# Loading the raw A tiles of a Strassen stage 6.5 products ahead instead of 9, in a one-core Mamba-2/GLA layer

## The chip, the cores and the metric

One core of a Trainium2 chip. The metric is the device time of one execution in microseconds, as the median of several runs. The change is judged by whether that time goes down, stays or goes up.

## The reference, cut to what matters

The kernel computes one layer of a hybrid decoder: 2048 tokens and 16 meta tokens in front of them, of width 1024, float32. A root-mean-square norm feeds one wide input projection; from it come a Mamba-2 (SSD) branch with a causal convolution and a chunked scan, a gated linear attention (GLA) branch, and two merge gates. Each branch output goes through a 1024 by 1024 projection, is multiplied by the sigmoid of its gate, and the sum goes through an output projection onto the residual, with a last norm:

```
u = rmsnorm(h, norm_w)
z, xbc, dt, q, k, v, g, a_lr, merge_g = split(u @ w_in)
y_ssd = norm(ssd(conv(xbc), dt) * silu(z))
y_gla = norm(gla(q, k, v, log_sigmoid(a_lr @ w2 + b))) * silu(g)
gates = sigmoid(merge_g)                    # two of them
merged = gates0 * (y_ssd @ w_br0) + gates1 * (y_gla @ w_br1)
out = rmsnorm(h + merged @ w_out, final_norm_w)
```

The last four lines' products, from `merge_g` on, are what the second half of the kernel computes, and where most of the change lies.

## The kernel before, in words

**Number format.** Every float32 operand is split into a high and a low part of the faster type fp32r: ACT copies the raw tile into the high part, and DVE or POOL subtracts it from the raw tile for the low part. A product is then three matmuls, L190 (high by high), L191 and L192 (the cross terms). A tile is not ready for TensorE (PE) until it is loaded (SP issues the DMA), copied (ACT) and subtracted.

**Phase 1 (0 to about 1500 us).** Four blocks of 512 tokens; in each, eight units of input projections (four SSD, four GLA) on PE, with the scans of earlier units run beside them. Weights come through `load_w`: a raw tile `wr` by DMA, ACT L170 for the high part, POOL L171 for the low part, both into `whl`; the first time, the split weight is also stored to DRAM (`k_...`, by `save`), and from then on it is loaded split. In block 0 every weight is split this way. Besides its own weights, block 0 also prepares the six weights of the first gate products (`EARLY`, products 1 and 2 of three column groups), one behind each of the units 0 to 5; they are needed only at the end of phase 1. The order of the instructions of PE and SP is the order of the program here; the other engines' order is set by a planner.

**Phase 2 (about 1525 us to the end).** Seven stages: two of gates (gate1, gate0), four of branches (br00, br10, br01, br11) and the output stage. Each multiplies 2 by 2 blocks with the Winograd form of Strassen's algorithm: seven products P1 to P7, in the order 1, 2, 6, 7, 5, 3, 4, the weights as A and the tokens as B (in the output stage the tokens as A and the weights as B). A stage has four or eight column groups n, taken in pairs: P1 of the even n, P1 of the odd n, P2 of both, and so on, 14 products to a pair. A product is 12 matmuls.

- A: `load_a` (L948) loads four raw tiles `ar` of a group (a11, a21, a22, a12, 256 KB each; eight buffers, so two groups). `sum_a` (L957 to L960) makes the sums on POOL, three into tiles `as` and one over a21. `prep_a` splits what a product needs into `a` (ACT L968, DVE L969). P1, P2 and P4 use raw tiles a11, a12, a22, so a buffer of `ar` is free once the last of its splits is done; a22 is split last, for P4.
- B: `load_b` (L936) loads a raw tile `br` (five buffers), `prep_b` splits it into `b1` to `b7` (ACT L941, DVE L942), 28 tiles per stage.
- Products accumulate in banks: P1, P6, P5, P3 in a bank `pj`, with P1, P6 and P5 each copied out by ACT (`sn`, L989) before the next product enters the same bank. P7 and P4 use `pt`, P2 uses `pc`.
- `fetch` loads gates or partial sums into `io` (L1034, L1038; L1062 in the output stage, where the buffers are first stored as the result), and ACT's queue stores finished tiles (L1158). `make_sums` prepares sums of B for later stages.

SP's order is by hand in phase 2 as well, the order of the other engines is the planner's. The place of a load in SP's order is set by a position counted in products: `at(pos, fn)` puts it down, and after product i the entries of positions i to i+1 are run in order of position. A load stands at `i - LOAD` for the first product i of a group (one product later for odd n). Since the odd group's own first product is one later too, that is 9 products ahead for the even group and 7 behind that pair's start for the odd. The split `prep_a` stands `AHEAD` products in front of its product; the loads of a stage's 28 B tiles begin 16 positions ahead of their stage (12 and 4 more), 0.8 of a position apart.

SP issues loads one after the other, and each waits for its own buffer to be free, so a load that waits holds all loads behind it.

**The passage.** The last phase-1 steps run early products of the first gate stage: P1 and P2 of n = 0, 1, 2 and P6 of n = 0 and 1, from weights and sums kept in SBUF. Then the pools of phase 1 on the right side of SBUF are released, and pools of phase 2 are opened in their place (`bops7`, `bops5`, `raws`, `aops`, `outs`, `small`), so that the first tiles of phase 2 wait for the last uses of phase-1 tiles at the same addresses (among them `acc`, `act`, `cin`, `tok` and `g`). The first entries run at position -1: A of n = 0 and 1, then B of P7 and P5.

```
at(first_at.get(n, i - LOAD + (n % 2)), lambda st=st, n=n: load_sum_a(st, n))
...
def load_sum_a(st, n):
    st.load_a(n)
    st.sum_a(n)
```

## Time and profile before

| | |
|---|---|
| runs | 2344.55, 2331.62, 2341.62 us, median 2341.62 |
| profiled execution | 2336.1 us, span 2334.3 us, mean granted TensorE clock 0.990 |
| PE busy | 2251.8 us, 96% of the span |
| PE weight loads | 1949.7 us, 84% |
| DVE busy | 1556.3 us, 67% |
| ACT busy | 1184.6 us, 51% |
| POOL busy | 696.6 us, 30% |
| DMA moved | 528.56 MB, mean 226 GB/s |

PE matmul and PEld (the weight loads of the array) overlap. A line names an instruction's place in the code, its engine, its output and inputs, how many there were, their busy time and mean duration in ns, and after the bar the idle time of the engine in front of them with what ended most of it. `SPq` rows are the sequencer that issues DMAs, with the time that it waited. In a timeline a row is start, duration, instruction, and in square brackets the idle time before it and what released it. The granted clock is 1.00 at full speed and 0.50 at half.

### The profile page before, as it was taken

The page shows a single profiled execution, that of the slowest core. Times are in us where ns is not written, and L with a number is a line of the kernel's source. Part 1 is how long each engine was busy: PE and PEld are TensorE (multiplying, and loading weights), DVE is VectorE, ACT ScalarE, POOL GpSimd, SP SyncE. Part 2 cuts the span into 40 slices and gives each one's busy share as a digit, 9 for nine tenths or more (in the row PEclk, how much of TensorE's full clock was granted, in tenths as well). Part 3 has the DMA queues.
Part 4 walks back from the last instruction along what each step waited for, and adds up shares of the span by engine and source line. Part 5 has one row for each costly group of instructions (what it writes and reads, how often), then busy time and mean ns, then how long its engine had stood idle before and what let it go on. Part 6 is the DMA issues. An engine that isn't in the chain of part 4 may idle for free.

```text
span 2334.3 us, 36553 instructions
## 1 busy us (share of the span) xinstructions
PE 2251.8 (96%) x12641; PEld 1949.7 (84%) x12641; DVE 1556.3 (67%) x2893; ACT 1184.6 (51%) x2762; POOL 696.6 (30%) x691
## 2 busy tenths in 40 slices
PE   7899999999999999999999999979999999999998
PEld 6899988888889989888988898858788778777786
DVE  5677766676675676576667556655644778887875
ACT  4666655465544455544455534444644644453543
POOL 3444533122222122211212101046354333423241
PEclk9999999999999999999999999989999999999999
DMA  8766966667785676786666656468765778877753
GB/s 297 246 214 227 323 234 206 224 195 240 239 283 186 213 222 213 265 275 201 206 222 217 204 170 200 131 212 257 245 208 183 237 250 285 285 277 246 245 166 110
DMA packets 305579, 528.56 MB, mean 226 GB/s; under 512 B 28144, under 2 KB 144112, under 8 KB 305392
## 3 DMA queue, kind: packets, MB, share of 16 engines
q1 hardware_dynamic: 204432, 413.33, 54.0%
q10 hardware_dynamic: 100960, 112.88, 13.9%
q8 instruction: 99, 1.62, 0.3%
q14 instruction: 88, 0.72, 0.1%
HBM read 375.76 MB, written 150.34 MB: 225 GB/s over the span
## 4 chain that ended last, share of the span: by engine, by line
PE 42%; DMA 12%; DVE 7%; issue 4%; ACT 4%; POOL 2%; SPq 2%; ACTq 0%; POOLq 0%; DVEq 0%
PE pj L190 9%; PE pj L192 9%; PE pj L191 9%; DMA br<-br_t 2%; DVE b L942 2%; PE pt L191 1%; PE pt L192 1%; DVE a L969 1%; PE pt L190 1%; DMA acc<-in_xmt 1%; PE pc L190 1%; PE pc L192 1%; PE pc L191 1%; PE pc L708 1%; DMA io<-g 1%
## 5 line engine op out<-in xcount | busy, mean ns | idle before, releaser
L190 PE MATMUL pj<-u,whl 128*128 128x512 f32 (+1 forms) x1196 | 453.6, 379 | 15.3 <-ACT g_all L442 6.2
L192 PE MATMUL pj<-u,whl 128*128 128x512 f32 (+1 forms) x1196 | 437.4, 366 | 1.1 <-POOL whl L171 0.6
L191 PE MATMUL pj<-u,whl 128*128 128x512 f32 (+1 forms) x1196 | 436.2, 365 | 0.0
L190 PE MATMUL pj<-whl,u 128*128 128x256 f32 (+1 forms) x992 | 289.3, 292 | 2.0 <-ACT u L303 2.0
L192 PE MATMUL pj<-whl,u 128*128 128x256 f32 (+1 forms) x992 | 282.7, 285 | 1.4 <-DVE u L305 1.4
L191 PE MATMUL pj<-whl,u 128*128 128x256 f32 (+1 forms) x992 | 282.5, 285 | 0.2 <-POOL whl L171 0.2
L190 PEld LDWEIGHTS pj<-u,whl 128*128 128x128 f32 x1196 | 228.9, 191 | 54.1 <-ACT acc L480 7.1
L192 PEld LDWEIGHTS pj<-u,whl 128*128 128x128 f32 x1196 | 228.4, 191 | 37.8 <-POOL whl L171 1.6
L191 PEld LDWEIGHTS pj<-u,whl 128*128 128x128 f32 x1196 | 229.2, 192 | 33.7
L190 PE MATMUL pj<-b,a 128*128 128x512 f32 x620 | 242.9, 396 | 10.5 <-ACT sn L989 9.1
L192 PE MATMUL pj<-b,a 128*128 128x512 f32 x620 | 243.9, 394 | 3.0 <-DVE a L969 3.0
L191 PE MATMUL pj<-b,a 128*128 128x512 f32 x620 | 244.1, 394 | 1.0 <-DVE b L942 1.0
L171 POOL TENSOR_TENSOR whl<-wr,whl 128x512 fp32r<-128x512 f32 (+1 forms) x106 | 142.9, 1356 | 184.3 <-ACT whl L170 146.0
L942 DVE TENSOR_TENSOR b<-br,b 128x512 fp32r<-128x512 f32 x196 | 157.7, 828 | 59.2 <-ACT b L941 56.0
L190 PEld LDWEIGHTS pj<-whl,u 128*128 128x128 f32 x992 | 190.1, 192 | 3.4 <-ACT u L303 2.6
L80 POOL TENSOR_TENSOR wr<-wr 128x256 f32<-128x256 f32 x80 | 65.8, 822 | 425.9 <-DMA wr<-u 172.8
L192 PEld LDWEIGHTS pj<-whl,u 128*128 128x128 f32 x992 | 190.0, 192 | 1.9 <-DVE u L305 1.9
L191 PEld LDWEIGHTS pj<-whl,u 128*128 128x128 f32 x992 | 190.3, 192 | 0.9 <-POOL whl L171 0.4
L957 POOL TENSOR_TENSOR as<-ar,ar 128x512 f32<-128x512 f32 x40 | 63.2, 1580 | 405.0 <-DMA ar<-in_w_br 192.7
L969 DVE TENSOR_TENSOR a<-ar,a 128x512 fp32r<-128x512 f32 x154 | 133.0, 878 | 75.6 <-ACT a L968 74.9
L941 ACT ACTIVATE b<-br 128x512 fp32r<-128x512 f32 x196 | 119.9, 627 | 119.1 <-DMA br<-br_t 46.0
L484 DVE SCALAR_TENSOR_TENSOR acc<-cin,hcw,acc 128x512 f32<-128x512 f32 (+1 forms) x192 | 153.8, 801 | 30.0 <-ACT acc L480 29.1
(290 smaller groups left out, 5061.2 us busy)
## 6 DMA issues: line engine op xcount, KB each, us to landing
whl<-k_s SPq DMA_DIRECT2D x96, 512.0 KB, 4.3
whl<-k_g SPq DMA_DIRECT2D x96, 512.0 KB, 4.1
whl<-k_v SPq DMA_DIRECT2D x48, 512.0 KB, 3.8
wr<-in_w_feat SPq DMA_DIRECT2D x72, 256.0 KB, 4.3
whl<-k_z SPq DMA_DIRECT2D x36, 512.0 KB, 3.7
k_s<-whl SPq DMA_DIRECT2D x32, 512.0 KB, 3.7
cb<-cumd ACTq DMA_DIRECT2D x64, 256.0 KB, 5.5
y<-gg ACTq DMA_DIRECT2D x64, 256.0 KB, 4.4
```

The lines of the kernel that those rows point to most:

```text
L80: nc.gpsimd.tensor_tensor(o, x, y, op=ALU.subtract)
L171: nc.gpsimd.tensor_tensor(hl[:, 1], raw, hl[:, 0].bitcast(F32), op=ALU.subtract)
L190: nc.tensor.matmul(ps, sh, mh, start=first, stop=False, **kw)
L191: nc.tensor.matmul(ps, sh, ml, start=False, stop=False, **kw)
L192: nc.tensor.matmul(ps, sl, mh, start=False, stop=last, **kw)
L484: nc.vector.scalar_tensor_tensor(acc, cin[:, k:k + tt], hcw[:, ti, k:k + 1], acc, op0=ALU.mult, op1=ALU.add)
L708: nc.tensor.matmul(ps[:, r * P:(r + 1) * P], kq[:, 2 * r * P:(2 * r + 1) * P], kq[:, (2 * r + 1) * P:(2 * r + 2) * P], start=True, stop=True)
L941: nc.scalar.activation(t[:, 0], raw, AF.Copy)
L942: nc.vector.tensor_tensor(t[:, 1], raw, t[:, 0].bitcast(F32), op=ALU.subtract)
L957: nc.gpsimd.tensor_tensor(s1, a21, a22, op=ALU.add)
L969: nc.vector.tensor_tensor(t[:, 1], src, t[:, 0].bitcast(F32), op=ALU.subtract)
```

## The change

Four edits. First, in block 0 the six early gate weights come behind units 2 to 7 instead of units 0 to 5. Second, tiles `as` move from the pool `raws` to a pool of their own (`sums`), and tiles `io` from the pool `outs` to a pool of their own (`ios`), both opened ahead of `raws`; the same numbers of buffers. By that the tiles lie at other addresses: `io` over phase 1's `acc`, `cb`, `c1` and `cin`, `ar` over `act` and `cin` (before, over `acc` and `cb`), and the first five `a` where `io` and a part of `a` lay; `as` stay. Third, LOAD becomes 6.5, so that a group's raw tiles of A are placed 6.5 products (even n) ahead of the pair's first product or 4.5 (odd n) instead of 9 and 7. Since `prep_a` of P4, in front by AHEAD = 5, is placed at 7 and 6 products ahead of the pair's first product, the load of A now stands behind the split of a22, in the order of the program, and not in front of it. Fourth, in the first gate stage the four B tiles of P7 are placed ahead of A of n = 0 and 1.

The number of instructions on every engine stays the same, and so does PE's order in phase 1. In phase 2 the groups of four loads of A move on SP: at a stage's start three loads of B (the tenth to twelfth) come in front of the even group and three more in front of the odd group, and in places two fetches of `io` or four loads of `make_sums` too.

```diff
@@ phase 1, block 0
-            if b == 0 and i < len(EARLY):
-                load_w(*gate_w(*EARLY[i]))
+            if b == 0 and i >= 2:
+                load_w(*gate_w(*EARLY[i - 2]))
@@ sum_a
-            s1, s2, s4 = [mk(rpl, [P, 4, P], F32, "as", bufs=6) for _ in range(3)]
+            s1, s2, s4 = [mk(asl, [P, 4, P], F32, "as", bufs=6) for _ in range(3)]
@@ io
-        return mk(opl, [P, BLK], F32, "io", bufs=8)
+        return mk(iol, [P, BLK], F32, "io", bufs=8)
@@ the order of phase 2
-    AHEAD, LOAD = 5, 9
+    AHEAD, LOAD = 5, 6.5
...
-            first_at = {0: -1, 1: -0.99, 3: 2, 2: 3} if st is stages[0] else {}
+            first_at = {0: -0.99, 1: -0.985, 3: 2, 2: 3} if st is stages[0] else {}
...
-    begins_b = {7: -0.98, 5: -0.9, 3: 0.5, 4: 1.8, 1: 3.2, 2: 4.4, 6: 5.6}
+    begins_b = {7: -1, 5: -0.9, 3: 0.5, 4: 1.8, 1: 3.2, 2: 4.4, 6: 5.6}
@@ make_sums of later stages
-                        yield from make_sums(opl, "io", 8, *sums[key], j, c, nc.scalar)
+                        yield from make_sums(iol, "io", 8, *sums[key], j, c, nc.scalar)
@@ the pools of phase 2
+    asl, iol = pool2("sums", 1, side="right"), pool2("ios", 1, side="right")
     rpl = pool2("raws", 1, side="right")
```

Lines behind 1182 of the changed kernel are one further down.

## The prediction

> **What bounds the kernel now.** I read the engines' busy times first, then the stretches, then the waits, and only then the instructions around the waits that cost something.

> The page, its span, its engine table and two groups of matmuls:

> ```profile
> span 2334.3 us, 36553 instructions
> PE 2251.8 (96%) x12641; PEld 1949.7 (84%) x12641; DVE 1556.3 (67%) x2893; ACT 1184.6 (51%) x2762; POOL 696.6 (30%) x691
> L190 PE MATMUL pj<-u,whl 128*128 128x512 f32 (+1 forms) x1196 | 453.6, 379 | 15.3 <-ACT g_all L442 6.2
> L190 PE MATMUL pj<-b,a 128*128 128x512 f32 x620 | 242.9, 396 | 10.5 <-ACT sn L989 9.1
> ```

> TensorE is the bound: 2334.3 - 2251.8 = 82.5 us are idle. The change removes no matmul, so it can win back only idle time and time at the halved clock. The stretches where it acts (columns: length, busy time of each engine, granted clock, DMA share, GB/s):

> ```profile
> 103.00:116.30 13.30, 10.40 (x78) 9.66 (x79) 12.48 (x26) 7.74 (x21) 7.14 (x8) 1.00 0.69 226
> 116.30:119.70 3.40, 3.40 (x17) 3.40 (x17) 0.97 (x3) 1.98 (x4) 0.13 (x1) 0.50 0.82 275
> 1536.20:1546.40 10.20, 4.49 (x8) 2.35 (x9) 6.58 (x5) 4.41 (x7) 10.04 (x8) 0.50 0.70 248
> 1550.00:1578.00 28.00, 24.87 (x96) 18.54 (x97) 22.68 (x30) 17.80 (x34) 12.34 (x8) 0.94 0.75 253
> 1600.00:2200.00 600.00, 588.13 (x2528) 473.49 (x2527) 424.27 (x571) 295.14 (x531) 234.79 (x180) 1.00 0.74 248
> ```

> Three places: block 0 (an idle of some 3 us and 3.4 us at half clock behind it), the passage from phase 1 to phase 2 at 1525 to 1578, and the 600 us of stages with 11.9 us idle. What TensorE waits for between 1600 and 2200 is nearly all of that 11.9:

> ```profile
> PE pj L190 <- ACT sn L989: 8.7, 10, 2.2
> PE pj L192 <- DVE a L969: 3.0, 3, 1.4
> ```

> A product may not enter the pj bank until ACT has copied the one before out of it (the snapshot, L989). So I asked what ACT waits for from 1600 on, and what SP's queue waits for from 1510 on:

> ```profile
> ACT b L941 <- DMA br<-br_t: 46.0, 26, 7.1
> ACT b L941 <- DMA br<-out_t: 21.7, 11, 7.3
> ```
> ```profile
> SPq L948 <- DVE a L969: 143.6, 41, 11.5
> SPq L936 <- DVE b L942: 112.4, 84, 13.4
> SPq L1062 <- DMA out_h<-io: 58.2, 13, 13.5
> SPq L948 <- DMA g<-acc: 22.1, 1, 22.1
> ```

> ACT waits for tiles of B (br), and SP, which loads them, stands for 143.6 us in front of loads of A (L948) whose buffers a split (L969) has not freed. One case shows the chain whole. SP, ACT and PE around 2059 to 2092 (start, duration, instruction, in brackets the idle before it):

> ```profile
> 2052.11 1.87 SPq L948 DMA_DIRECT2D ar<-in_w_br  x4
> 2058.59 9.73 SPq L948 DMA_DIRECT2D ar<-in_w_br  x4
> 2068.85 0.42 SPq L936 DMA_DIRECT2D br<-br_t  x1
> ```
> ```profile
> 2072.75 0.63 ACT L941 ACTIVATE b<-br 128x512 fp32r<-128x512 f32 x1 [7.13 <-DMA br<-br_t]
> 2073.29 0.58 ACT L989 ACTIVATE sn<-pj 128x512 f32<-128x512 f32 x1
> 2091.50 0.60 ACT L989 ACTIVATE sn<-pj 128x512 f32<-128x512 f32 x1 [0.91 <-DVE io L1045]
> ```
> ```profile
> 2073.92 0.50 PE L190 MATMUL pj<-b,a 128*128 128x512 f32 x1 [1.33 <-ACT sn L989]
> 2074.26 0.39 PE L191 MATMUL pj<-b,a 128*128 128x512 f32 x1
> 2074.49 0.40 PE L192 MATMUL pj<-b,a 128*128 128x512 f32 x1
> ```

> SP needs 9.73 us for four issues of A; the br behind them goes out at 2068.85; ACT stands 7.13 us for it, with the snapshot next in its order; PE loses 1.33 us.

> **Part 1, the six gate weights of block 0, two units later.** Each has one 256 KB load, one ACT copy, one POOL subtraction, one 512 KB store. ACT in block 0, and the waits of PE there (80 to 330):

> ```profile
> 113.89 0.63 ACT L170 ACTIVATE whl<-wr 128x512 fp32r<-128x512 f32 x1 [1.85 <-DMA k_m<-whl]
> 114.43 0.46 ACT L442 ACTIVATE g_all<-pj,pv 128x264 f32<-128x264 f32 x1
> ```
> ```profile
> PE pj L190 <- ACT g_all L442: 6.2, 2, 3.6
> PE pj L190 <- ACT acc L480: 5.7, 3, 4.1
> ```

> ACT waits 1.85 us for a store of such a weight, copies the next (0.63), and only then empties the bank for PE. With six weights moved, the second of the two g_all waits (6.2 - 3.6 = 2.6 us) can go, and with it the 3.4 us at half clock at 116.3, in which 1.7 us of matmul time is lost: 4.3 us at most. Against it: the weights now come behind units 2 to 7, where they meet the other waits (acc, up to 4.1); two more ACT copies and two POOL subtractions fall into the last units, 2 x 0.63 and 2 x 1.36 (the POOL row is below), both engines under 60% busy there, so 0 to 1 us on the path. If cover is missing, the same 1.85 + 0.63 appears at another unit, and a half window with it: +1. From -5 to +1 I take -3, nearer the row that vanishes. SP's stores of these tiles move along; the order of PE's work in block 0 is the same.

> **Part 2, the passage.** SP, POOL, DVE and PE at 1530 to 1556, and one POOL group of the page:

> ```profile
> 1530.75 3.65 SPq L948 DMA_DIRECT2D ar<-in_w_feat  x8
> 1534.51 1.90 SPq L936 DMA_DIRECT2D br<-gate_t  x4
> 1555.86 1.85 SPq L948 DMA_DIRECT2D ar<-in_w_feat  x4
> ```
> ```profile
> 1535.30 1.26 POOL L957 TENSOR_TENSOR as<-ar,ar 128x512 f32<-128x512 f32 x1 [12.33 <-DMA ar<-in_w_feat]
> ```
> ```profile
> 1540.82 8.62 DVE L942 TENSOR_TENSOR b<-br,b 128x512 fp32r<-128x512 f32 x7
> 1549.36 0.68 DVE L969 TENSOR_TENSOR a<-ar,a 128x512 fp32r<-128x512 f32 x1
> ```
> ```profile
> 1540.66 0.79 PE L190 MATMUL pt<-b,a 128*128 128x512 f32 x1 [8.49 <-ACT b L941]
> ```
> ```profile
> L171 POOL TENSOR_TENSOR whl<-wr,whl 128x512 fp32r<-128x512 f32 (+1 forms) x106 | 142.9, 1356 | 184.3 <-ACT whl L170 146.0
> ```

> Before, the first load of A waits 22.1 us for a store of phase 1 (g<-acc), whose tile lay where A goes; all eight go out at 1530.75, the four b7 loads behind them. After, four b7 loads go first: about 1.9 us earlier than now by program order alone, and the new addresses of A (over other tiles of phase 1) make A wait for the stores of y as well as g. The first A still waits until about 1530 to 1532, so POOL starts about 1533.3 instead of 1535.3 (-2). P7 of n=0 may start at 1539 to 1542. P7 of n=1 needs all eight POOL sums, and four more DVE splits now stand between: 8 x 1.26 + 13 x 0.68 = 18.9 us if one waits for the other, from 1533.3, is 1552; the same sum before (8 x 1.26 + 9 x 0.68 = 16.2 from 1535.3) gives 1551.5 where the trace has 1550.0, so 1550.7: no earlier. What does come earlier is the loads of A for n=3, which stand behind the splits (about 1550 instead of 1556); those are late now: of the 28.0 - 24.87 = 3.1 us idle in 1550 to 1578, most lies there. With the halved clock before 1578 I put 4 us to it. Against that, P7 of n=0 earlier leaves a longer hole in front of n=1, and up to 2 us more at half clock. Net -2, from -8 (the whole 8.49 shrinks by 4 and the 4 us go) to +3.

> [...]

> **Part 3, A loaded 6.5 instead of 9 products ahead.** A product takes 12 matmuls; their starts are 0.23 us apart (2074.26 to 2074.49 above), so 2.73 us. The load now stands behind the split of P4's a22 of the pair before in program order, so that SP reaches it after that buffer is free, and the three br loads for the next stage that stood behind a blocked A stand ahead of it. In the case above br then leaves at about 2059 instead of 2068.85; the 7.13 us of ACT are gone, the snapshot at about 2071, PE does not wait. Each wait costs more than its idle: the matmul before it lasts 0.39 to 0.40 us where 0.23 passes in a row, 0.16 per wait. Thirteen waits: 8.7 + 3.0 + 13 x 0.16 = 13.8 us. The snapshot share is 8.7 + 1.6 = 10.3, all at the ends of pairs of stages with ACT in a br wait where I followed it; the 3.5 us of the a-split waits follow from the same late ACT or from POOL's sums. I take 11 of 13.8; from -14 to -3 (only the cases with a long br wait).

> What it costs: A comes later. A group needs 5 us to land, four POOL sums and a split before its first sum is of use:

> ```profile
> ar<-in_w_br SPq DMA_DIRECT2D x64, 256.0 KB, 5.3
> L957 POOL TENSOR_TENSOR as<-ar,ar 128x512 f32<-128x512 f32 x40 | 63.2, 1580 | 405.0 <-DMA ar<-in_w_br 192.7
> ```

> 5.3 + 4 x 1.58 + 0.63 + 0.68 = 12.9 us. The group issued at 2052.11 belongs to the pair whose first snapshot is at 2091.50, less a product 2088.8: a lead of 36 us; the one that began at 2058.59 and ended at 2068.3 has 20. 2.5 products later is 6.8 us less at most, 13 for the worst: enough, barely, and the worst one was late only because it was blocked. No cost on the path. If that cover fails, see the slower rival. In the out stage two fetches that wait for stores (up to 13.5 us) now stand ahead of the group; the lead there is of the same size, so at most 1 us.

> **Part 4, pools.** Own pools for sums and io move addresses only: io lies over acc, cb and cin of phase 1, freed before 1530. Nothing, if the fetches of the first gates do not wait for those; cover 20 us.

> **Sum**: -3 - 2 - 11 = -16 us against the profiled execution's 2336.1 us (span plus 1.8): 2320.1. That execution lies 5.5 under the median of the runs shown, 2341.62, so on the median's basis 2325.6. I say 2324.

> **Rivals.**
> *No change that can be measured* (0.5% of 2341.6, 11.7 us, is about what a measurement of this kernel tells from none). SP stays blocked: it only runs until some other buffer is not free, since L936 waits for DVE 112.4 us as well, and a br that leaves earlier meets that. Then the snapshot waits stay; gain 0 to 8: about 2336. For it: the even and odd groups of A need four buffers that the same splits free. Against: at 2058.59 the buffers of br were free and SP stood at L948.

> *Slower.* A's later place is too late. The place leaves 6.5 x 2.73 = 17.7 us for the even n and 5.5 x 2.73 = 15.0 for the odd, against 12.9 needed. If SP goes in step with PE instead of ahead of it and is held once per pair by a br as now (7.3 us), PE stands 7.3 - 4.8 = 2.5 us for the even and 5.2 for the odd, some 4 per pair of n; 11 such pairs, less the 16 gained: +28, about 2368. It decides from the point where SP reaches a group less than 13 us before P1. Against: leads of 20 to 36 us at 2052 to 2091.

> [...]

> **How the numbers follow.** My forecast 0.56, no change 0.25, the passage worse 0.09, slower 0.10. Faster by over 0.5% (below 2329.9): 0.54 of the first, 0.05 of the passage: 0.60 with 0.01 of the rest. Slower (above 2353.3): 0.09. The remainder 0.31. The range: low end -8 - 5 - 14 = -27, from the median 2315, less 9 for runs as far under it as 2331.62 is under 2341.62: 2306; high end the no-change case with a run at the upper 2344.55: 2345. Slower lies outside (0.09). The likeliest case alone: 2312 to 2334.

> **What would show it.** Part 1: no L170 wait for k_m before 114 and no 0.50 clock at 116 to 120. Part 2: b7 loads ahead of ar, POOL's first sum at 1533, n=3's ar at about 1550. Part 3: SPq L948 <- DVE a below 50 us, ACT's br_t and out_t waits halved, the ten snapshot waits down to two or three. Wrong if these waits stay, if POOL or ACT waits for ar at the head of a pair, or if the half clock shows at new places.

## The result, and the profile after

The change makes the kernel faster, by less than half of what was forecast and by less than the 0.5% taken as the bound: median 2333.22 us (2323.27 to 2337.84, 22 runs) against 2341.05 us (2331.62 to 2348.85, 22 runs), ratio 0.9966, 95% interval 0.9957 to 0.9976, that is 7.9 us. The forecast was 2324 with a range of 2306 to 2345, which holds the time, and 0.60 on a gain of more than 0.5%; the 0.34% that came is the "no measurable change" of its cases, though these 22 runs do tell it from none.

The page of the changed kernel, its span and engines:

```profile
span 2334.1 us, 36595 instructions
PE 2252.7 (97%) x12641; PEld 1954.5 (84%) x12641; DVE 1569.1 (67%) x2893; ACT 1185.7 (51%) x2762; POOL 698.4 (30%) x691
```

This execution took 2335.9 us, no less than the profiled one of before (2336.1): it lies at the upper end of its runs. Phase 1 hides the gain in it. The first snapshot of an early gate product, which PE reaches after the same work in both kernels, starts at (timeline of ACT, before and then after)

```profile
1501.40 0.60 ACT L989 ACTIVATE acc<-pj 128x512 f32<-128x512 f32 x1 [1.93 <-PE pj L192]
```
```profile
1508.02 0.60 ACT L989 ACTIVATE acc<-pj 128x512 f32<-128x512 f32 x1 [1.91 <-PE pj L192]
```

6.6 us later, while what follows it takes 2334.1 - 1508.0 = 826.1 us instead of 2334.3 - 1501.4 = 832.9. Over the 17 traces of this study (the two here, and one of each kernel below) that first snapshot lies anywhere from 1501.4 to 1513.1, with and without the moved weights. So the time from it to the end, called phase 2 below, is compared trace by trace, and the whole by medians. One trace of phase 2 is one draw as well: run 8's is 8.6 us shorter than that of before, though its twelve times show no gain, and runs 7, 9 and 10 were profiled in the fastest of their executions. Where the two disagree, the times decide.

Stretches of PE (before, then after; the passage, the first 10 us behind it, and the stages):

```profile
1495.00:1600.00 105.00, 89.78 (x398) 69.62 (x399) 64.11 (x93) 52.59 (x112) 40.00 (x30) 0.93 0.59 196
1600.00:1610.00 10.00, 10.00 (x45) 8.05 (x44) 2.84 (x4) 3.66 (x8) 9.37 (x10) 1.00 0.48 153
```
```profile
1495.00:1600.00 105.00, 91.13 (x413) 72.24 (x412) 73.19 (x109) 53.63 (x117) 42.80 (x32) 0.93 0.63 211
1600.00:1610.00 10.00, 7.79 (x26) 5.89 (x27) 4.46 (x5) 4.44 (x8) 9.76 (x10) 0.83 0.48 155
1600.00:2200.00 600.00, 591.30 (x2543) 478.68 (x2544) 425.49 (x570) 297.61 (x530) 225.58 (x175) 1.00 0.74 248
```

The passage has 13.9 us of idle instead of 15.2, but behind it there is a new hole, 2.2 us idle and the clock at 0.83. The 600 us of stages have 8.7 us idle instead of 11.9, the 2.2 us of the new hole among them. The waits in them, and SP's and ACT's waits that the prediction named:

```profile
PE pj L190 <- ACT sn L989: 5.6, 3, 2.2
PE pj L190 <- ACT a L968: 3.0, 1, 3.0
PE pj L192 <- DVE a L969: 1.0, 2, 0.7
```
```profile
SPq L936 <- DVE b L942: 159.6, 97, 16.0
SPq L948 <- DVE a L969: 52.2, 21, 9.8
```
```profile
ACT b L941 <- DMA br<-br_t: 25.2, 16, 4.0
ACT b L941 <- DMA br<-out_t: 12.0, 9, 3.5
```

The middle of the chain did as forecast: SP's waits in front of A fell from 143.6 to 52.2 us, ACT's for tiles of B from 67.7 to 37.2, the snapshot waits from ten to three. TensorE got back 3.2 us of the 11 counted on.

The new hole is one wait. ACT, POOL and PE of the changed kernel near 1600:

```profile
1600.35 0.52 ACTq L83 DMA_DIRECT2D br_t<-io  x1
1601.26 0.63 ACT L968 ACTIVATE a<-ar 128x512 fp32r<-128x512 f32 x1 [6.26 <-POOL io L80]
```
```profile
1592.43 1.30 POOL L957 TENSOR_TENSOR as<-ar,ar 128x512 f32<-128x512 f32 x1
1597.09 1.75 POOL L960 TENSOR_TENSOR as<-ar,as 128x512 f32<-128x512 f32 x1
1598.80 0.72 POOL L80 TENSOR_TENSOR io<-io 128x256 f32<-128x256 f32 x1
```
```profile
1601.94 0.50 PE L190 MATMUL pj<-b,a 128*128 128x512 f32 x1 [3.02 <-ACT a L968]
```
```profile
1603.90:1607.30 3.40, 3.40 (x10) 2.65 (x9) 1.88 (x3) 2.51 (x5) 3.40 (x3) 0.50 0.40 121
```

ACT's queue holds a store (L83) of the sums of B that POOL makes for a later stage; POOL makes the four sums of A (1592.43 to 1598.84) first, and the split of A that PE needs stands behind that store on ACT. PE loses 3.0 us and then half of 3.4 (at half clock its matmuls start 0.43 us apart, 0.23 behind it). Runs 5 and 9 ask what brings this about.

### The profile page after: what moved, and what is told of

It is laid out like the page before. It is cut to its first block, busy times and chain, and to the rows that moved or that the text cites. A ratio compares the mean times of both kernels' runs of the same rounds, so it can differ in the third digit from the quotient of the medians.

```text
span 2334.1 us, 36595 instructions
## 1 busy us (share of the span) xinstructions
PE 2252.7 (97%) x12641; PEld 1954.5 (84%) x12641; DVE 1569.1 (67%) x2893; ACT 1185.7 (51%) x2762; POOL 698.4 (30%) x691
## 4 chain that ended last, share of the span: by engine, by line
PE 41%; DMA 5%; DVE 3%; issue 1%; ACT 1%; POOL 1%; SPq 0%; ACTq 0%; DVEq 0%; POOLq 0%
PE pj L192 9%; PE pj L190 9%; PE pj L191 9%; PE pt L192 2%; PE pt L191 2%; PE pt L190 2%; PE pc L190 1%; PE pc L191 1%; PE pc L192 1%; DMA br<-out_t 1%; DVE b L942 1%; PE pc L708 1%; DMA io<-p 1%; PE pc L569 1%; DMA m<-io 0%
## 5 line engine op out<-in xcount | busy, mean ns | idle before, releaser
L190 PE MATMUL pj<-u,whl 128*128 128x512 f32 (+1 forms) x1196 | 454.8, 380 | 14.3 <-ACT acc L480 6.2
L192 PE MATMUL pj<-u,whl 128*128 128x512 f32 (+1 forms) x1196 | 438.2, 366 | 1.7 <-POOL whl L171 0.8
L191 PE MATMUL pj<-u,whl 128*128 128x512 f32 (+1 forms) x1196 | 437.0, 365 | 0.0
L190 PE MATMUL pj<-whl,u 128*128 128x256 f32 (+1 forms) x992 | 289.9, 292 | 1.5 <-ACT u L303 1.5
L192 PE MATMUL pj<-whl,u 128*128 128x256 f32 (+1 forms) x992 | 283.0, 285 | 1.6 <-DVE u L305 1.6
L191 PE MATMUL pj<-whl,u 128*128 128x256 f32 (+1 forms) x992 | 282.8, 285 | 0.3 <-POOL whl L171 0.3
L190 PEld LDWEIGHTS pj<-u,whl 128*128 128x128 f32 x1196 | 229.2, 192 | 53.9 <-ACT acc L480 7.6
L192 PEld LDWEIGHTS pj<-u,whl 128*128 128x128 f32 x1196 | 228.4, 191 | 38.5 <-POOL whl L171 2.1
L191 PEld LDWEIGHTS pj<-u,whl 128*128 128x128 f32 x1196 | 229.4, 192 | 34.0
L190 PE MATMUL pj<-b,a 128*128 128x512 f32 x620 | 242.8, 396 | 8.7 <-ACT sn L989 5.6
L192 PE MATMUL pj<-b,a 128*128 128x512 f32 x620 | 244.6, 395 | 1.1 <-DVE a L969 1.0
L191 PE MATMUL pj<-b,a 128*128 128x512 f32 x620 | 244.7, 395 | 0.0
L171 POOL TENSOR_TENSOR whl<-wr,whl 128x512 fp32r<-128x512 f32 (+1 forms) x106 | 143.4, 1361 | 185.3 <-ACT whl L170 149.5
L969 DVE TENSOR_TENSOR a<-ar,a 128x512 fp32r<-128x512 f32 x154 | 144.9, 948 | 79.6 <-ACT a L968 78.8
L190 PEld LDWEIGHTS pj<-whl,u 128*128 128x128 f32 x992 | 190.4, 192 | 2.8 <-ACT u L303 1.8
L192 PEld LDWEIGHTS pj<-whl,u 128*128 128x128 f32 x992 | 190.2, 192 | 2.3 <-DVE u L305 2.3
L191 PEld LDWEIGHTS pj<-whl,u 128*128 128x128 f32 x992 | 190.6, 192 | 1.0 <-POOL whl L171 0.5
L942 DVE TENSOR_TENSOR b<-br,b 128x512 fp32r<-128x512 f32 x196 | 159.6, 840 | 30.7 <-ACT b L941 30.3
L957 POOL TENSOR_TENSOR as<-ar,ar 128x512 f32<-128x512 f32 x40 | 57.7, 1441 | 379.7 <-DMA ar<-in_w_br 194.7
L941 ACT ACTIVATE b<-br 128x512 fp32r<-128x512 f32 x196 | 118.2, 625 | 80.0 <-DMA br<-br_t 25.2
## 6 DMA issues: line engine op xcount, KB each, us to landing
wr<-in_w_feat SPq DMA_DIRECT2D x72, 256.0 KB, 4.7
cb<-cumd ACTq DMA_DIRECT2D x64, 256.0 KB, 5.7
y<-gg ACTq DMA_DIRECT2D x64, 256.0 KB, 4.4
```

What stands on the lines that cost most here:

```text
L171: nc.gpsimd.tensor_tensor(hl[:, 1], raw, hl[:, 0].bitcast(F32), op=ALU.subtract)
L190: nc.tensor.matmul(ps, sh, mh, start=first, stop=False, **kw)
L191: nc.tensor.matmul(ps, sh, ml, start=False, stop=False, **kw)
L192: nc.tensor.matmul(ps, sl, mh, start=False, stop=last, **kw)
L941: nc.scalar.activation(t[:, 0], raw, AF.Copy)
L942: nc.vector.tensor_tensor(t[:, 1], raw, t[:, 0].bitcast(F32), op=ALU.subtract)
```

## The experiments

All ratios are to runs of the kernel before on the same chip. Theories and rivals have letters, given in the expectations; where a run overturned one, the text behind it says so.

### The three parts one by one

Run 1, the six weights alone:

```diff
-            if b == 0 and i < len(EARLY):
-                load_w(*gate_w(*EARLY[i]))
+            if b == 0 and i >= 2:
+                load_w(*gate_w(*EARLY[i - 2]))
```

> Only the six gate weights of block 0 move two units later; everything else is as before. Theory A (the whole change's 7.9 us come mostly from the place of A in the stages): ratio 0.9985 to 1.000, that is 0 to 3.5 us, from the g_all wait at 115 that shrinks from 2.6 to about 1.3 us and its 3.4 us at half clock; the idle of TensorE between 1600 and 2200 stays 11 to 13 us. Theory B (the gain comes from block 0, and the stages give back at 1602 what they win): ratio 0.996 to 0.9975, 6 to 9 us, with the same 11 to 13 us idle in 1600 to 2200.

Measured: 0.9992 (0.9976 to 1.0007), phase 2 830.7 us. No gain that can be told; theory B falls. The idle from 1600 to 2200, 9.4 us, is under what both theories said, with the same phase 2 as before.

Run 2, the pools (with `as` and `io` made in them, as in the change) and P7's B first, LOAD 9:

```diff
+    asl, iol = pool2("sums", 1, side="right"), pool2("ios", 1, side="right")
-            first_at = {0: -1, 1: -0.99, 3: 2, 2: 3} if st is stages[0] else {}
+            first_at = {0: -0.99, 1: -0.985, 3: 2, 2: 3} if st is stages[0] else {}
-    begins_b = {7: -0.98,
+    begins_b = {7: -1,
```

> Only the pools of the sums and of io and the order of P7's B ahead of A; LOAD stays 9. Theory A: the passage gains nothing, since A still waits for the stores of phase 1 and P7 of n=1 still needs all sums: ratio 0.9985 to 1.0015, POOL's first sum about 2 us later behind the last phase-1 snapshot than before or equal. Theory C (the new addresses and the earlier b7 carry the gain): ratio 0.996 to 0.998, and the idle of TensorE between 1525 and 1600 some 4 us less than the 14.0 us of before.

Measured: 0.9967 (0.9955 to 0.998), phase 2 827.0. Theory A is wrong here: the passage part alone wins as much as the whole change. Theory C has the ratio; the idle from 1525 to 1600 fell by 2.9 us (to 11.1) rather than 4, and the stages have 7.2 us instead of 11.9, which neither theory named.

Run 3, LOAD alone:

```diff
-    AHEAD, LOAD = 5, 9
+    AHEAD, LOAD = 5, 6.5
```

> Only LOAD 6.5 instead of 9. Theory A: ratio 0.9965 to 0.998, 5 to 8 us; SP's waits in front of A for a split fall from 144 to about 50 us, the snapshot waits from ten to three or four. The wait of ACT at 1602 behind a store of the sums (6.3 us, 3.0 us of TensorE) is there too. Theory B: ratio 0.999 to 1.001, what the stages win is given back at 1602 and by later waits. Theory C: LOAD alone is of no use without the pools: ratio 1.000 to 1.003.

Measured: 0.9966 (0.9952 to 0.998), phase 2 822.0: as much as the whole change again, so theory C falls as to LOAD alone. Its stages are nearly closed, and there is no stall at 1602:

```profile
1600.00:2200.00 600.00, 597.44 (x2577) 482.90 (x2576) 436.95 (x576) 300.84 (x536) 237.47 (x181) 1.00 0.76 250
```

Run 4, the whole change without the weights (against the changed kernel):

```diff
-            if b == 0 and i >= 2:
-                load_w(*gate_w(*EARLY[i - 2]))
+            if b == 0 and i < len(EARLY):
+                load_w(*gate_w(*EARLY[i]))
```

> The whole change without the move of the six weights. Theory A: ratio 0.997 to 0.9985, at most 3 us slower than the whole change. Theory B: 0.999 to 1.001. The second look at phase 2 of the whole change shows whether its stall at 1602 (3.0 us of TensorE, ACT behind POOL) and its three snapshot waits come again (theory A: they do, at the same places).

Measured: 0.9979 (0.9967 to 0.9991), phase 2 825.5. A hole behind the passage comes again, 2.8 us of the 10 behind 1600, this time as two waits of 1.4 us, one for a split of A and one for a snapshot.

So two parts that win 0.33% each win no more together. One of them takes away what the other gives.

### What is lost between the two parts

Run 5, the changed kernel with A of the first stage at 9:

```diff
-            at(first_at.get(n, i - LOAD + (n % 2)), ...
+            at(first_at.get(n, i - (9 if st is stages[0] else LOAD) + (n % 2)), ...
```

> The changed kernel with A of the first stage at 9 products again, the other six stages at 6.5. Theory D (the gain of the passage, some 3 to 5 us, is lost in the changed kernel because A of the first stage's third pair now stands behind the sums of B on POOL, and ACT behind a store of those sums): the stall at 1602 goes, TensorE's idle between 1525 and 1650 falls by 3 us or more against the changed kernel, the stages behind 1650 stay as in it; ratio 0.994 to 0.9955. Rival E (the stall at 1602 hides another that was there anyway): ratio 0.996 to 0.9975, and an idle of 2 to 3 us turns up at another product before 1650.

Measured: 0.9949 (0.9931 to 0.9968), phase 2 820.6, 5.5 us less than the changed kernel. Of the stall, 0.8 us is left:

```profile
PE pj L190 <- ACT sn L989: 4.0, 3, 2.3
PE pj L190 <- ACT a L968: 0.8, 1, 0.8
```

The stall goes and the ratio lies in theory D's range, though its interval overlaps that of the whole change (0.9957 to 0.9976), and so the time alone does not decide. Run 9 below limits what D says of the cause.

### What in the passage wins

Run 7, the pools alone (again with `as` and `io` in them; the order of the loads as before), and run 8, P7's B first alone:

```diff
+    asl, iol = pool2("sums", 1, side="right"), pool2("ios", 1, side="right")
```
```diff
-            first_at = {0: -1, 1: -0.99, 3: 2, 2: 3} if st is stages[0] else {}
+            first_at = {0: -0.99, 1: -0.985, 3: 2, 2: 3} if st is stages[0] else {}
-    begins_b = {7: -0.98,
+    begins_b = {7: -1,
```

> Only the two pools: other addresses, same order. Theory D: the eight loads of A now wait for the stores of y as well and go out later or equal, with P7's B behind them: ratio 0.999 to 1.002, the passage between 1500 and 1600 as before or up to 2 us worse. Rival H (the addresses carry the gain of the passage): ratio 0.9965 to 0.998.

> Only P7's B loaded ahead of A, with the pools as before. Theory D: b7 is split before POOL's sums are done, P7 of n=0 waits for A only and the waits of the later products for B at 1570 to 1575 go: ratio 0.9965 to 0.9985. Rival H: nothing without the new addresses, since A waits 22 us for g<-acc in front or behind: ratio 0.999 to 1.001.

Measured: the pools alone 0.9976 (0.9962 to 0.999), phase 2 822.2; P7 first alone 0.9991 (0.9975 to 1.0007), phase 2 824.3. Rival H's ratios fit both runs, and theory D as to the passage is wrong: what gain can be told comes with the addresses. Where it arises is only partly clear: the idle of run 7 from 1600 to 2200 is also lower, 7.5 instead of 11.9 us, and what the addresses do there was not followed. SP with the pools alone, and its PE at the passage:

```profile
1516.12 21.30 SPq L948 DMA_DIRECT2D ar<-in_w_feat  x8
```
```profile
1541.63 0.80 PE L190 MATMUL pt<-b,a 128*128 128x512 f32 x1 [4.77 <-ACT b L941]
1549.12 0.50 PE L190 MATMUL pt<-b,a 128*128 128x512 f32 x1 [1.48 <-ACT a L968]
```

and the same of the changed kernel:

```profile
1518.43 13.73 SPq L936 DMA_DIRECT2D br<-gate_t  x4
1532.21 9.03 SPq L948 DMA_DIRECT2D ar<-in_w_feat  x8
```
```profile
1545.83 0.79 PE L190 MATMUL pt<-b,a 128*128 128x512 f32 x1 [7.05 <-ACT a L968]
1554.44 0.51 PE L190 MATMUL pt<-b,a 128*128 128x512 f32 x1 [2.41 <-ACT a L968]
```

At the new addresses the first load of A leaves at 1516, 10 us behind the first snapshot (1506.1 there); the eight take 21.30 us, since later ones still wait for phase 1. The four loads of b7 put in front of it need 13.7 us, because they wait for phase 1 themselves, so A leaves at 1532, 24 us behind the first snapshot. The first hole is 7.05 instead of 4.77 us, and what PE waits for is A instead of B.

Run 9, the changed kernel with A of n = 0 and 1 first again, and run 10, that with the first stage at 9:

```diff
-            first_at = {0: -0.99, 1: -0.985, 3: 2, 2: 3} if st is stages[0] else {}
+            first_at = {0: -1, 1: -0.99, 3: 2, 2: 3} if st is stages[0] else {}
-    begins_b = {7: -1,
+    begins_b = {7: -0.98,
```

> The changed kernel with A of n=0 and 1 loaded ahead of P7's B again, as before; weights, pools and LOAD 6.5 as changed. Theory I (the new addresses let A of n=0 go out at 1516 to 1522, ten us before phase 1 ends, and the b7 loads put ahead of it take that away again, since the second and the fourth of them wait for phase 1 themselves): first idle of the passage 5 us or less instead of 7.1, first A about 8 us behind the first snapshot instead of 24, ratio 0.9935 to 0.9955. Rival J (the stall at 1602 depends on the passage and eats the gain however that goes): ratio 0.996 to 0.9975.

> As the run with A first, and A of the first stage at 9 products. Theory I and D: no stall near 1602 and the early A: ratio 0.9925 to 0.9945, 13 to 17 us, the fastest of all. Rival J: no better than either alone, 0.995 to 0.996.

Measured: 0.9937 (0.9918 to 0.9955), phase 2 818.0; and 0.9919 (0.99 to 0.9938), phase 2 815.7, median 2324.34 us against 2343.8. Run 10 is the fastest kernel here, faster than the changed one by its interval. Its passage and stages:

```profile
1495.00:1600.00 105.00, 94.40 (x420) 73.78 (x420) 63.34 (x99) 55.48 (x116) 43.05 (x33) 0.95 0.62 204
1600.00:2200.00 600.00, 597.60 (x2582) 484.14 (x2581) 435.54 (x586) 301.08 (x539) 234.80 (x180) 1.00 0.74 250
```

10.6 us idle in the passage instead of 13.9, 2.4 in the stages instead of 8.7. Theory I holds in place and sign: at the new addresses the first hole is 4.6 to 5.2 us where A goes first and 7.05 to 7.65 where it doesn't. Over all traces, counted from 24 to 100 us behind the first snapshot, PE is idle for 9.0 to 9.8 us with the new addresses and A first (runs 7, 9, 10, 11, 15), for 11.1 to 14.2 with the new addresses and b7 first (runs 2, 4, 5 and the changed kernel), and for 12.7 to 15.1 at the old addresses.

In time the order is less sure. With LOAD 6.5, A first wins about 0.3% (run 9 against the whole change, whose intervals just miss each other, and run 10 against run 5, whose intervals overlap a little). With LOAD 9, run 2 (b7 first) has 0.9967 and run 7 (A first) 0.9976, the other way and inside the intervals.

Rival J's bound falls, but its premise, that the stall at 1602 depends on the passage, is right. Run 9 leaves the first stage at 6.5, POOL makes its four sums in one piece there as well (1591.21 to 1597.28), and yet PE does not wait:

```profile
1595.00:1615.00 20.00, 20.00 (x88) 16.24 (x87) 10.62 (x12) 9.88 (x17) 18.74 (x19) 1.00 0.77 251
```

Run 3, with the old passage and LOAD 6.5, has no such stall either. So it takes both, the later A of the first stage and b7 ahead of A; undoing either one removes it (0.8 us are left in run 5). By which step b7 first brings the split behind the store on ACT was not followed.

Run 11, run 10 with the fetches one product later:

```diff
-            at(i - 2, lambda st=st, n=n, p=p: st.fetch(n, *DONE[p]))
+            at(i - 1, lambda st=st, n=n, p=p: st.fetch(n, *DONE[p]))
```

> As the run before it, and the fetches of gates and partial sums one product ahead of the product that ends their block instead of two. Theory K (the two or three snapshot waits that LOAD 6.5 leaves between 2000 and 2200 come from SP standing at such a fetch, with br behind it): SP's waits of L1034 and L1038 for DVE L1049 fall below 10 us, the snapshot waits fall from 4 to 2 us or less; 1 to 3 us faster than the run before it. Rival L: the fetch then comes too late for its user, DVE waits for io, and PE for DVE or ACT: 2 us or more slower.

Measured: 0.9934 (0.9915 to 0.9952), phase 2 820.3. The snapshot waits do go (1.2 us in run 10, none here), but SP's waits at the fetches for DVE L1049 rise from 22.2 to 43.4 us, and PE waits 2.1 us for a split on ACT and 3.4 us for splits on DVE instead. Theory K falls; rival L fits, though the intervals of runs 10 and 11 overlap. No gain.

### What in the stages wins

Run 6, LOAD 7.5 alone:

```diff
-    AHEAD, LOAD = 5, 9
+    AHEAD, LOAD = 5, 7.5
```

> The kernel before with LOAD 7.5 instead of 9 and nothing else. Theory F (what counts is that the load of A comes behind the split that frees its buffers, at 7 products ahead, not that it comes later): at 7.5 the load still stands in front of it, so SP's waits in front of A for a split stay above 100 us, the snapshot waits between 1600 and 2200 come to 6 us or more; ratio 0.998 to 1.000. Rival G (every bit later helps in proportion): 1.5 of the 2.5 products give 60 percent, SP's waits about 90 us, ratio 0.9975 to 0.9985.

Measured: 0.9961 (0.9947 to 0.9975), phase 2 823.4, the whole gain of 6.5. SP's waits in front of A for a split are 76.6 us and the snapshot waits 1.8. Theory F, which is the prediction's account of part 3 (the load must come behind the split that frees its buffers), falls; so does G's proportion.

Run 12, only the odd group later, 4.5 products ahead of its pair's start instead of 7:

```diff
-            at(first_at.get(n, i - LOAD + (n % 2)), ...
+            at(first_at.get(n, i - (LOAD - 2.5 * (n % 2)) + (n % 2)), ...
```

> The kernel before with only the odd group's A later (4.5 products ahead of the pair, as in the changed kernel), the even group at 9 as before. Theory M (it is the odd group's two last loads that wait for the splits of a22, since the even group gets the four buffers that come free early): SP's waits in front of A for a split fall to 50 to 80 us, the snapshot waits to 2 to 4 us, ratio 0.9965 to 0.998, as with LOAD 6.5 alone or 7.5. Rival N (both groups count): waits above 100 us, ratio 0.998 to 1.000.

Measured: 1.0011 (0.9996 to 1.0027), phase 2 834.2. SP's waits fell as with LOAD 6.5 and nothing was won:

```profile
SPq L948 <- DVE a L969: 60.5, 29, 10.7
```
```profile
1600.00:2200.00 600.00, 588.50 (x2526) 474.11 (x2525) 437.33 (x565) 296.22 (x527) 235.77 (x181) 1.00 0.75 249
```

Theory M falls. Some snapshot waits went, and others came: one, of 2.8 us, for a split of A that stands on ACT behind a store which waits 2.5 us for DVE. Why the planner's order turns out so here was not followed further.

Run 13, only the even group later, to 7.5, and run 14, A as before and the loads of B earlier:

```diff
+            at(first_at.get(n, i - (LOAD if n % 2 else 7.5) + (n % 2)), ...
```
```diff
-            at(pos - (4 if si else ...
+            at(pos - (6.5 if si else ...
```

> The kernel before with only the even group's A later, at 7.5 products instead of 9, the odd group at 7 as before. Theory O (the odd group's place did nothing, so it is the even group's: two more tiles of B, the tenth and eleventh of the next stage, and a fetch go ahead of it): ratio 0.996 to 0.998, the snapshot waits between 1600 and 2200 at 2 to 5 us, although SP's waits for the splits of a22 stay above 100 us. Rival Q (both groups have to move together, because they are held by the same splits): ratio 0.999 to 1.001, snapshot waits 6 us or more.

> The kernel before with A as it was, and the loads of B of the six later stages 2.5 positions earlier. Theory O (B ahead of A is what counts, however it comes about): ratio 0.996 to 0.998, ACT's waits for br_t and out_t below 45 us together (68 before), snapshot waits at 2 to 5 us. Rival Q (it is A's own place behind its splits): ratio 0.999 to 1.002; SP's waits in front of A stay at 140 us, and five br buffers, held longer, give SP's waits for DVE b 150 us or more.

Measured: 0.9966 (0.9956 to 0.9976), phase 2 821.7; and 0.9958 (0.9942 to 0.9974), phase 2 822.2. Each wins as much as LOAD 6.5, and in each SP still stands over 100 us in front of A. Run 13, and then run 14:

```profile
SPq L948 <- DVE a L969: 114.3, 37, 10.5
```
```profile
1600.00:2200.00 600.00, 596.69 (x2577) 483.81 (x2576) 437.40 (x577) 302.73 (x542) 239.33 (x185) 1.00 0.75 252
```
```profile
SPq L948 <- DVE a L969: 107.6, 27, 12.5
```
```profile
1600.00:2200.00 600.00, 596.94 (x2579) 484.37 (x2578) 445.52 (x583) 300.85 (x541) 243.82 (x186) 1.00 0.75 251
```

Theory O fits runs 3, 6, 12, 13 and 14: what counts is that two or three more tiles of B have left SP before A blocks it, not how long A blocks it. ACT's waits are no price either: for br_t it waits 46.7 us in run 13, against 46.0 before. How the gain comes about was followed at one place only. ACT at the change of stages near 1915, before:

```profile
1912.73 0.63 ACT L941 ACTIVATE b<-br 128x512 fp32r<-128x512 f32 x1 [6.26 <-DMA br<-br_t]
1913.27 0.58 ACT L989 ACTIVATE sn<-pj 128x512 f32<-128x512 f32 x1
...
1915.62 0.63 ACT L941 ACTIVATE b<-br 128x512 fp32r<-128x512 f32 x1 [1.25 <-DMA br<-br_t]
1916.98 0.63 ACT L941 ACTIVATE b<-br 128x512 fp32r<-128x512 f32 x1 [0.73 <-DMA br<-br_t]
...
1917.52 0.58 ACT L989 ACTIVATE sn<-pj 128x512 f32<-128x512 f32 x1
```

and at the same place in run 13:

```profile
1918.27 0.63 ACT L941 ACTIVATE b<-br 128x512 fp32r<-128x512 f32 x1 [6.06 <-DMA br<-br_t]
1918.81 0.58 ACT L989 ACTIVATE sn<-pj 128x512 f32<-128x512 f32 x1
...
1921.16 0.63 ACT L941 ACTIVATE b<-br 128x512 fp32r<-128x512 f32 x1 [1.26 <-DMA br<-br_t]
1921.70 0.58 ACT L989 ACTIVATE sn<-pj 128x512 f32<-128x512 f32 x1
```

ACT waits as long as before for the first late tile (6.06 against 6.26 us), but only one B split instead of two stands between the two snapshots, so the second comes 2.9 instead of 4.3 us behind the first.

Run 15, run 10 with the other stages at 7.5:

```diff
-    AHEAD, LOAD = 5, 6.5
+    AHEAD, LOAD = 5, 7.5
```

> The fastest so far (A of n=0 and 1 ahead of P7's B, first stage at 9) with the other stages at 7.5 instead of 6.5. If the place behind the even split matters by itself: 2 us slower or more, 0.993 to 0.994. If 7.5 does the same as 6.5, as it did alone: ratio 0.991 to 0.993, idle of TensorE between 1600 and 2200 at 2 to 5 us.

Measured: 0.9938 (0.9917 to 0.9959), phase 2 818.2, 3.8 us idle in the stages. The ratio lies in the first range and the idle in the second, and the interval covers both; 6.5 and 7.5 can't be told apart.

## Why the prediction was wrong, step by step

The step that failed is the sum. It took three gains from three places as independent and put the cost of a later A at nothing. Measured alone, the parts come to 1.9 (run 1), 7.7 (run 2) and 8.0 us (run 3), 17.6 in all and near the 16 of the sum, though part by part they are not its 3, 2 and 11: that they add up to its number is luck. Together they give 7.9.

**Part 1, -3.** Alone it measures -1.9 us with an interval from -5.6 to +1.6, so the time neither shows nor refutes the term. The traces bear out its mechanism. The wait shrank from 2.64 to 1.28 us (before, then after):

```profile
114.94 0.39 PE L190 MATMUL pj<-u,whl 128*128 128x264 f32 x1 [2.64 <-ACT g_all L442]
```
```profile
110.55 0.39 PE L190 MATMUL pj<-u,whl 128*128 128x264 f32 x1 [1.28 <-ACT g_all L442]
```

A stretch at half clock that starts at 112 to 117 us is in all ten traces with the weights in the old order, and in one of the seven with the new. From the first to the last of block 0's 32 copies L479 on ACT, which empty PE's banks, it takes 173.9 to 176.5 us in the ten and 171.0 to 172.8 in the seven. But the first snapshot comes no earlier: its median is 1506.2 in the ten and 1507.4 in the seven. What takes the gain back in between was not followed. A smaller misreading: ACT is not under 60% busy in the last units, but 62% (55.77 of 90 us from 240 on).

**Part 2, -2, and part 4, nothing.** Alone the two measure -7.7 us, almost the low end of the range of part 2; with LOAD 6.5 in place they add nothing (8.0 us in run 3, 4.9 in run 4). The reasons were upside down. The prediction read that A's new addresses make it wait for more stores, and priced the pools at nothing. A does wait for the stores of y (12.6 us in run 7), but behind its first loads, and the pools alone win 5.6 us (2.3 to 8.9), with A's first load 10 us behind the first snapshot instead of 29 (1530.75 - 1501.4). It took b7 first as the gain; b7 first holds A back by waits of its own (A at 24 us behind the snapshot). "The loads of A for n=3 come earlier" held, counted from the first snapshot: 47.7 us (1555.68 - 1508.02) instead of 54.5. PE's waits behind 1570, though, were for B (0.81 and 1.00 us before), and they are gone wherever b7 goes first. The failing step is "the first A still waits until about 1530 to 1532", true of the changed order, and not of the addresses.

**Part 3, -11.** The mechanism had the right end and the wrong lever. That B late at ACT delays the snapshot is right; that A must stand behind its freeing split is wrong (runs 6, 12, 13, 14). The size failed twice. First, the base: 11.9 us of idle in 1600 to 2200 is the most of all traces with LOAD 9 in every stage and B unmoved; run 1, with the same phase 2, has 9.4, and runs 2, 7 and 8, with other addresses or another passage, have 7.2, 7.5 and 6.9. With 2.6 left in run 3, the term is 4 to 9 us, and run 3's ratio says 8.0 (4.7 to 11.2), so that alone the 11 is at the upper edge. Second, "no cost on the path": the reading that four loads of sums in front of A do no harm looked at leads to P1 in later stages, and not at the first stage, where POOL carries both and ACT's queue has the stores. That is the slower rival's kind of mechanism, once instead of eleven times: 3.0 us of idle and 3.4 us at half clock. It is no cost of the later A alone (run 3 has none), but of the later A together with b7 first.

**The rivals.** "SP stays blocked" did not happen as told (52 us are left of 144), yet its time, 2336, is nearer than the forecast's, by luck. "The passage worse", given 0.09, is half there: against the pools alone, P7 of both n is later, with a second hole of 2.41 us instead of 1.48, and half clock as below for 10.2 us, as long as before. Between 1525 and 1600 both traces have 13.7 us at half clock, these 10.2 and 3.4 later (from 1573.8 before, from 1556.1, behind the second hole, after). That a longer second hole brings more half clock was the author's estimate; no run shows it.

```profile
1542.50:1552.70 10.20, 5.85 (x12) 3.64 (x12) 10.05 (x7) 4.42 (x7) 10.12 (x7) 0.50 0.71 233
```

**The sum** was to add up from three places taken one by one. Runs 2, 3 and 4 show that they don't add: 7.7 and 8.0 us alone (2343.43 x 0.0033 and x 0.0034), 4.9 together (x 0.0021). The low end of the range has a slip of 1 us: 2341.62 is 10 above 2331.62, not 9.

## What to carry to other kernels

A wait of a queue is not a price: more than halving SP's waits in front of A won nothing in one order (run 12) and leaving three quarters of them won everything in another (runs 13 and 14), so ask which instruction stands behind the wait, and how near its engine is to the one that counts (here the snapshot on ACT, next to PE, behind 6.26 us for a tile of B). Where a tile of the next phase is to be loaded early, look at what its address was used for last (at the new addresses A's first load left 10 us behind the first snapshot instead of 29), and try first in the queue the load that may leave first, and not the one that is needed first (a first hole of 4.6 to 5.2 us against 7.05 to 7.65). Two changes to one queue have to be tried together as well as alone, and one trace's idle is one draw: the stages whose repair was priced at 11 us had 11.9 and 9.4 us idle in two traces of the same phase 2.

## What the runs showed of the hardware that was not expected

Whether a hole halves the clock is not settled by its length. A hole of 1.95 us at 1064 in the changed kernel is followed by 3.4 us at half clock, one of 2.71 us at the same instruction before is not. The changed kernel:

```profile
1064.24 0.48 PE L806 MATMUL pc<-s_gla,act 128*128 128x256 f32 x1 [1.95 <-DVE s_gla L807]
```
```profile
1064.60:1068.00 3.40, 3.40 (x10) 2.63 (x9) 1.28 (x3) 2.06 (x9) 0.00 (x0) 0.50 0.00 0
```

The kernel before:

```profile
1059.73 0.48 PE L806 MATMUL pc<-s_gla,act 128*128 128x256 f32 x1 [2.71 <-DVE s_gla L807]
```

```profile
1061.20:1064.60 3.40, 1.45 (x11) 1.19 (x9) 3.23 (x9) 2.81 (x9) 0.00 (x0) 1.00 0.81 313
```
```profile
1054.97:1058.38 3.41, 2.04 (x15) 1.75 (x13) 3.27 (x10) 1.42 (x5) 0.00 (x0) 1.00 0.98 335
1058.38:1061.79 3.41, 2.06 (x9) 1.75 (x10) 2.94 (x6) 3.41 (x13) 0.00 (x0) 1.00 0.11 45
```

PE is idle for 1.95 us of the one step, and for 1.37 and 1.35 of the two. Over the 17 traces, from 30 us on, all 134 steps at full clock with more than 1.93 us idle were followed by a step at half clock, of the 190 with 0.98 to 1.93 us 29 were, and of the 10891 with less none.

In the changed kernel 1.95 us of the 3.41 were enough. With eight to eleven such stretches in a trace, of 3.4 to 13.7 us, this is one source of the spread of 12 us in which the first snapshot falls. Up to that snapshot PE is busy at half clock for 22.7 us in the trace of before and for 29.9 in that of the changed kernel; half of the difference, 3.6 us, is an estimate of the clock's share in the 6.6 us between the two. Over all traces that share was not measured.
